# RMS norms of a two-layer streaming encoder: one product with ones, and an inverse root at full width

## The chip, the cores and the metric

The kernel runs on one core of a Trainium2 chip. The metric is device time in microseconds (us) of one execution; the times shown are medians of several executions. The core has five engines that work side by side, each through its own queue in order: TensorE (PE, matrix products, with its weight loads shown apart as PEld), VectorE (DVE), ScalarE (ACT), GpSimd (POOL) and SyncE (SP, which issues the DMAs here).

## The reference, cut to what matters

A prompt of 1024 frames and a running stream of 32 frames go through two layers with d_model 1024. Layer 0 mixes by a gated recurrence (HGRN2), layer 1 by a sliding-window attention; both have a SwiGLU feed-forward part. Around each of these four parts stands an RMS norm on the way in and one on the way out, and the second layer's keys and values have a weight vector of their own on the same normalised x:

```python
def rms_norm(x, w):
    xf = x.astype(F32)
    y = xf * lax.rsqrt(jnp.mean(xf * xf, axis=-1, keepdims=True) + NORM_EPS)
    return (y * w.astype(F32)).astype(x.dtype)
...
for layer in range(DEPTH):
    h = rms_norm(x, norm_mix_pre[layer])
    ...
    x = x + rms_norm(mix, norm_mix_post[layer])
    hf = rms_norm(x, norm_ffn_pre[layer])
    a, b = jnp.split(hf @ w_ffn_in[layer], 2, axis=-1)
    x = x + rms_norm((jax.nn.silu(a) * b) @ w_ffn_out[layer], norm_ffn_post[layer])
```

In the recurrence each head's output has a norm over its 128 values too (`o = rms_norm(o, g_norm) * silu(g)`).

## The kernel before, in words

Activations lie transposed: the 1024 features in eight groups of 128 partitions, the 1056 frames along the free dimension in three blocks b = 0, 1, 2 of 384, 384 and 288 columns (`BL`). Each dense product splits both operands into a high and a low part (`wh`, `wl`, `xh`, `xl`) and adds three products, so eight feature groups make 24 matrix products into one PSUM tile (`mm_fm`, L133; `mm_tm` with frames on the output partitions, L145; `fmul`, L495, for the second feed-forward matrix). The PSUM pool of these tiles, `mmps()`, has four buffers. Weights come by DMA on SP into `wst` and are split by ACT (`wh`, L98 or L102) and DVE (`wl`, L99 or L103).

A norm needs, for each frame (column), the sum of squares over 1024 features, that is over eight groups and 128 partitions. `sq_acc` squares each group on ACT (L171, L174) and adds the groups on POOL (L175) into `acc`. Then come two steps:

- `rstd`: three products with blocks of 128 columns of `acc` as weights and one column of ones (L181) give the sums with frames on partitions, a tile of 128x3. `newton` (L152 to L161) makes the inverse root of it on DVE: 12 instructions on three columns, a first guess from the bits and three Newton steps. The result `r` (tiles `r2`, `rt`) is also what the products with frames on partitions use as scale of a row: in `vproj` (L702), `gproj` (L717, L718) and `vproj1` (L1121).
- `rbcast`: DVE makes a diagonal matrix `dm` from `ident` and `r` (L186), one product with ones as weights puts r on all partitions (L190), and ACT copies it from PSUM (L191) to `rb` or `rb2`, which scales columns.

There are 24 norms over d_model: three at the load of x (`xload`), and for each of the four parts and three blocks one of the part's output (in `postnorm`, with `rb2`), and one of the new x (in `postnorm`, with `rb`) except behind the last part. So twelve are of outputs and twelve of x. `gproj` uses `newton` too, on six columns, twelve times.

`postnorm` and the others are Python generators: a `yield` ends a piece, and the caller asks for pieces (`go`, `step`, `run`) between dense products, so the text gives an order of work in which norms and dense products interleave. `after_dense()` puts a norm's product in PE's queue behind the last dense product written before it. The tile framework then fixes each engine's order before the run by its own plan, in which an instruction that is ready in the plan may go ahead of one written earlier; on the chip each engine keeps to that order. In the first feed-forward part the second half of `postnorm` of block 2 goes on into the projections of the next layer (`go(f0)`).

Of the kernel before, what the change touches and what calls it, by code (L numbers as in the profile page):

```python
# [18 lines left out]
D = 1024  # L19
# [40 lines left out]
def build(nc, tc, I, O):  # L60
# [16 lines left out]
    def tt(tag, bufs):  # L77
        return tp.tile([128, 384], F32, tag=tag, name=tag, bufs=bufs)

    def mmps():  # L80
        return pm.tile([128, 512], F32, tag="mm", name="mm")
# [70 lines left out]
    def newton(dst, ss, n, cnt, wtag):  # L152
        v = tp.tile([128, n], F32, tag=wtag + "v", name="nv", bufs=2)
        t = tp.tile([128, n], F32, tag=wtag + "t", name="nt", bufs=2)
        nc.vector.tensor_scalar(v, ss, 1.0 / cnt, EPS, mult, add)
        nc.vector.tensor_scalar(dst.bitcast(I32), v.bitcast(I32), -0.5, float(0x5f3759df), mult, add)
        nc.vector.tensor_scalar(v, v, -0.5, None, mult)
        for _ in range(3):
            nc.vector.tensor_tensor(t, dst, dst, mult)
            nc.vector.tensor_tensor(t, t, v, mult)  # L160
            nc.vector.scalar_tensor_tensor(dst, t, 1.5, dst, add, mult)  # L161

    def newacc(b):
        acc = tt("acc", 3)
        if BL[b][1] < 384:
            nc.gpsimd.memset(acc[:, BL[b][1]:], 1.0)
        return acc
# [9 lines left out]
    def rstd(acc, r, ps=None):  # L177
        ps = mmps() if ps is None else ps
        with after_dense():
            for j in range(3):  # L180
                nc.tensor.matmul(ps[:, j:j + 1], acc[:, j * 128:(j + 1) * 128], ones[:, 0:1], start=True, stop=True)  # L181
        newton(r, ps[:, 0:3], 3, D, "n3")

    def rbcast(dst, r, W, ps=None):
        dm = tt("dm", 1).rearrange("p (a b) -> p a b", a=3)
        nc.vector.tensor_tensor(dm, ident.unsqueeze(1).broadcast_to([128, 3, 128]),  # L186
                                r.unsqueeze(2).broadcast_to([128, 3, 128]), mult)
        ps = mmps() if ps is None else ps
        with after_dense():
            nc.tensor.matmul(ps[:, :W], ones, dm.rearrange("p a b -> p (a b)")[:, :W], start=True, stop=True)  # L190
        nc.scalar.copy(dst[:, :W], ps[:, :W])  # L191
# [17 lines left out]
    def postnorm(b, mix, acc, w2, xold, wnext, spill, yout, done, more=None, full=None):  # L209
# [16 lines left out]
        r2 = tp.tile([128, 3], F32, tag="r2", name="r2", bufs=2)  # L226
        rstd(acc, r2)
        yield
        rb2 = tt("rb2", 1)
        rbcast(rb2, r2, W)  # L230
# [19 lines left out]
        if yout is None:  # L250
# [3 lines left out]
            r = cp.tile([128, 3], F32, tag=f"rt{b}", name=f"rt{b}")  # L254
            rstd(nacc, r)
            yield
            rb = cp.tile([128, W], F32, tag=f"rb{b}", name=f"rb{b}")
            rbcast(rb, r, W)
# [16 lines left out]
    def ffn(L, nx, post1, post, wmix, v1, w2, xold, wnext, spill, yout, res):  # L275
# [231 lines left out]
        def step(b):  # L507
            if b not in ts:
                c0, W = BL[b]

                def done(*r):
# [4 lines left out]
                                 lambda: mp.tile([128, 384], F32, tag="xo", name="xo", bufs=3))  # L516
# [130 lines left out]
    with tc.tile_pool(name="hp", bufs=1) as hp, \  # L647
# [4 lines left out]
        def xload(b, mid=None):  # L652
# [17 lines left out]
            yield  # L670
            r = rts[b] = cp.tile([128, 3], F32, tag=f"rt{b}", name=f"rt{b}")
            rstd(acc, r, hps.tile([128, 512], F32, tag="po", name="po", bufs=1) if b == 0 else None)
            yield
            rb = rbs[b] = cp.tile([128, W], F32, tag=f"rb{b}", name=f"rb{b}")
            rbcast(rb, r, W, hps.tile([128, 512], F32, tag="hs", name="hs", bufs=1) if b == 0 else None)
# [30 lines left out]
        def gproj(p, b):  # L706
# [3 lines left out]
            newton(ro, ssq[p, b], 6, 128, "n6")  # L710
# [13 lines left out]
        def stage_a(c, h, b):  # L724
# [16 lines left out]
            if h == b == 0:  # L741
                go(xl0)
                go(v0, 2)
                go(xl0)
            rb = rbs[b]
# [708 lines left out]
```

## Time and profile before

| | |
|---|---|
| median of 3 runs | 2577.68 us (2573.69 to 2578.14) |
| the profiled execution | 2575.38 us |
| its span, first to last instruction | 2573.6 us |
| PE, PEld busy | 2484.7, 2388.2 us (97%, 93%) |
| DVE, ACT, POOL busy | 1695.1, 1074.3, 453.9 us (66%, 42%, 18%) |
| chain that ended last | PE 77%, DVE 12%, ACT 4%, DMA 3% |
| mean granted TensorE clock | 0.986 |

How to read it: a row of a group names line, engine, operation, what is written and read (`out<-in`), the shape, the number of instructions, then busy time and mean ns of one, and the idle time of the engine before them with what ended it. A row of the timeline has the start and duration in us, and in brackets the idle time before it. [...] Products are pipelined and the ends of their records are modelled, so what a product costs PE is read from the distance of two starts. A row of waits says who waited for whom, us in total, how often, and the longest.

The dense work is steady from 725 to 1300 us and from 1880 to 2460 us (the first feed-forward matrices of the two layers). The recurrence fills the first 625 us, the attention 1480 to 1800.

### The profile page before, as it was taken

What the parts mean: (1) busy time and instruction counts of PE and PEld (TensorE: products, weight loads), DVE (VectorE), ACT (ScalarE), POOL (GpSimd) and SP (SyncE); (2) the same over time, 40 slices, a digit from 0 to 9 for tenths busy, and PEclk for the clock granted to TensorE, in tenths of its full rate; (3) what the DMA queues carried; (4) which work ended last, traced back from release to release, by engine and by line L of the source; (5) the groups of instructions that cost most, each with busy time, mean ns of one, the idle gap of its engine ahead of it and who ended that gap; (6) DMA issues with size and microseconds to landing.
All of it is one profiled execution on the core that took longest, in us unless ns stands there. A gap on an engine that the chain in (4) does not pass through costs nothing.

```text
span 2573.6 us, 44368 instructions
## 1 busy us (share of the span) xinstructions
PE 2484.7 (97%) x17232; PEld 2388.2 (93%) x17232; DVE 1695.1 (66%) x3694; ACT 1074.3 (42%) x2323; POOL 453.9 (18%) x652
## 2 busy tenths in 40 slices
PE   7999998999999999999998999989999999999997
PEld 7999998998899999999998997768899999999997
DVE  8787779888676666552467647687776666652455
ACT  6555655656433333342344324555433333342332
POOL 5543434332200000000034311121300000000021
PEclk9999999999999999999999999999999999999998
DMA  5333333443422222252455542223422222252454
GB/s 169 91 100 99 119 100 124 131 129 120 137 80 83 75 75 75 80 172 75 149 164 173 168 140 75 68 79 100 147 81 82 75 75 75 78 174 75 150 172 144
DMA packets 124155, 288.01 MB, mean 112 GB/s; under 512 B 13432, under 2 KB 68632, under 8 KB 123944
## 3 DMA queue, kind: packets, MB, share of 16 engines
q1 hardware_dynamic: 123944, 285.17, 35.1%
q8 instruction: 135, 2.21, 0.4%
q14 instruction: 76, 0.62, 0.1%
HBM read 237.25 MB, written 48.07 MB: 111 GB/s over the span
## 4 chain that ended last, share of the span: by engine, by line
PE 77%; DVE 12%; ACT 4%; DMA 3%; issue 2%; POOL 2%; SPq 0%; POOLq 0%; ACTq 0%; DVEq 0%
PE mm L133 28%; PE mm L495 17%; PE mm L404 15%; PE c L404 6%; PE mm L145 5%; DVE wl L103 2%; PE sc L1218 1%; PE pav L1276 1%; ACT wh L102 1%; PE ptp L1258 1%; DVE wl L99 1%; PE mm L190 1%; DVE mixb L240 1%; DMA xl<-g 1%; DVE mixb L239 1%
## 5 line engine op out<-in xcount | busy, mean ns | idle before, releaser
L133 PE MATMUL mm<-xh,wh 128*128 128x384 f32 (+1 forms) x1968 | 634.4, 323 | 8.1 <-ACT xh L206 7.1
L133 PE MATMUL mm<-xh,wl 128*128 128x384 f32 (+1 forms) x1968 | 626.5, 318 | 12.2 <-DVE wl L103 8.4
L133 PE MATMUL mm<-xl,wh 128*128 128x384 f32 (+1 forms) x1968 | 628.6, 319 | 1.0 <-DVE xl L207 0.8
L175 POOL TENSOR_TENSOR acc<-acc,tmp 128x384 f32<-128x384 f32 (+1 forms) x168 | 212.0, 1266 | 1724.6 <-ACT tmp L174 1721.3
L103 DVE TENSOR_TENSOR wl<-wst,wh 128x1024 fp32r<-128x1024 f32 (+1 forms) x301 | 377.2, 1255 | 183.2 <-ACT wh L102 182.3
L102 ACT CAST wh<-wst 128x1024 fp32r<-128x1024 f32 (+1 forms) x301 | 314.0, 1046 | 398.4 <-PE mm L495 231.8
L133 PEld LDWEIGHTS mm<-xh,wl 128*128 128x128 f32 x1968 | 373.4, 190 | 20.0 <-DVE wl L103 9.3
L133 PEld LDWEIGHTS mm<-xh,wh 128*128 128x128 f32 x1968 | 374.1, 190 | 15.2 <-ACT xh L206 7.1
L133 PEld LDWEIGHTS mm<-xl,wh 128*128 128x128 f32 x1968 | 373.9, 190 | 9.9 <-issue 3.9
L495 PE MATMUL mm<-xh,wl 128*128 128x384 f32 (+1 forms) x768 | 247.5, 322 | 1.7 <-DVE wl L103 1.7
L495 PE MATMUL mm<-xl,wh 128*128 128x384 f32 (+1 forms) x768 | 247.5, 322 | 0.0
L495 PE MATMUL mm<-xh,wh 128*128 128x384 f32 (+1 forms) x768 | 247.1, 322 | 0.0
L145 PE MATMUL mm<-wh,xh 128*128 128x256 f32 (+1 forms) x648 | 185.6, 287 | 1.9 <-ACT vt L702 1.9
L145 PE MATMUL mm<-wh,xl 128*128 128x256 f32 (+1 forms) x648 | 183.2, 283 | 0.0
L145 PE MATMUL mm<-wl,xh 128*128 128x256 f32 (+1 forms) x648 | 182.6, 282 | 0.0
L388 ACT CAST sh<-sr 128x512 fp32r<-128x512 f32 x144 | 89.5, 622 | 175.6 <-PE mm L404 147.9
L495 PEld LDWEIGHTS mm<-xh,wl 128*128 128x128 f32 x768 | 144.2, 188 | 2.1 <-DVE wl L103 2.1
L495 PEld LDWEIGHTS mm<-xh,wh 128*128 128x128 f32 x768 | 144.1, 188 | 0.0
L495 PEld LDWEIGHTS mm<-xl,wh 128*128 128x128 f32 x768 | 144.1, 188 | 0.0
L145 PEld LDWEIGHTS mm<-wh,xh 128*128 128x128 f32 (+1 forms) x648 | 119.0, 184 | 3.5 <-ACT vt L702 2.1
L145 PEld LDWEIGHTS mm<-wh,xl 128*128 128x128 f32 (+1 forms) x648 | 119.0, 184 | 0.8
L145 PEld LDWEIGHTS mm<-wl,xh 128*128 128x128 f32 (+1 forms) x648 | 118.5, 183 | 0.5
(278 smaller groups left out, 5113.3 us busy)
## 6 DMA issues: line engine op xcount, KB each, us to landing
wst<-in_wfo SPq DMA_DIRECT2D x92, 512.0 KB
wst<-in_wfi SPq DMA_DIRECT2D x88, 512.0 KB
wst<-in_wfq SPq DMA_DIRECT2D x47, 512.0 KB
g<-u SPq DMA_DIRECT2D x72, 192.0 KB
wst<-in_wi SPq DMA_DIRECT2D x24, 512.0 KB
wst<-in_wg SPq DMA_DIRECT2D x24, 512.0 KB
wst<-in_wao SPq DMA_DIRECT2D x24, 512.0 KB
xl<-g SPq DMA_DIRECT2D x32, 384.0 KB
```

Source lines behind the costliest of these rows:

```text
L99: nc.vector.scalar_tensor_tensor(wl[:, s], st[:, s], pcol(name, k0 + k), wh[:, s].bitcast(F32), mult, sub)
L102: nc.scalar.copy(wh[:, s], st[:, s])
L103: nc.vector.tensor_tensor(wl[:, s], st[:, s], wh[:, s].bitcast(F32), sub)
L133: last_mm[0] = nc.tensor.matmul(ps[:, :W], w, x, start=i == 0, stop=i == n - 1)
L145: last_mm[0] = nc.tensor.matmul(ps[:rows, :256], x, w, start=i == 0, stop=i == n - 1)
L175: nc.gpsimd.tensor_tensor(acc[:, :W], acc[:, :W], q[:, :W], add)
L190: nc.tensor.matmul(ps[:, :W], ones, dm.rearrange("p a b -> p (a b)")[:, :W], start=True, stop=True)
L239: nc.vector.scalar_tensor_tensor(m, m, pcol(w2, k), rb2[:, :W], mult, mult)
L240: nc.vector.tensor_tensor(m, m, xos[k][:, :W], add)
L388: nc.scalar.copy(h, r)
L404: last_mm[0] = nc.tensor.matmul(ps[:, :384], a, c, start=start and k == i == 0, stop=k == 3 and i == 2, skip_group_check=True)
L495: last_mm[0] = nc.tensor.matmul(ps[:, :W], a, c[:, q, :], start=start and q == i == 0, stop=stop and q == f - 1 and i == 2, skip_group_che ...
```

## The change

`rstd` and `rbcast` go. `rnorm` makes one product with ones (128x128) as weights and all columns of `acc`, which gives the sums on all partitions at once, and `rsqrt` makes the inverse root there at the width of the block: v = ss/1024 + eps and two squares and one linear step on ACT, the first guess and five more instructions on DVE, with a step of third order and a Newton step. The tile `dm` goes, and u, an intermediate, is written into the norm's PSUM tile by ACT. Where a scale of rows is needed (at the load of x, and with `tok=True` behind the first feed-forward part), `rcol` takes it out of the full-width result by products with one column of `ident` and a copy on DVE. `gproj` uses `rsqrt` with all steps on DVE. The columns of `acc` beyond a block's width aren't set to one any more. At the first head, `rcol` and the second piece of `vproj` change places with the broadcast.

```diff
-    def newton(dst, ss, n, cnt, wtag):
-        v = tp.tile([128, n], F32, tag=wtag + "v", name="nv", bufs=2)
-        t = tp.tile([128, n], F32, tag=wtag + "t", name="nt", bufs=2)
-        nc.vector.tensor_scalar(v, ss, 1.0 / cnt, EPS, mult, add)
+    def rsqrt(dst, ss, v, t, u, cnt, sq, lin):
+
+        lin(v, ss, 1.0 / cnt, EPS)
         nc.vector.tensor_scalar(dst.bitcast(I32), v.bitcast(I32), -0.5, float(0x5f3759df), mult, add)
-        nc.vector.tensor_scalar(v, v, -0.5, None, mult)
-        for _ in range(3):
-            nc.vector.tensor_tensor(t, dst, dst, mult)
-            nc.vector.tensor_tensor(t, t, v, mult)
-            nc.vector.scalar_tensor_tensor(dst, t, 1.5, dst, add, mult)
+        sq(t, dst)
+        nc.vector.tensor_tensor(t, t, v, mult)
+        lin(u, t, 0.375, -1.25)
+        nc.vector.tensor_tensor(t, u, t, mult)
+        nc.vector.scalar_tensor_tensor(dst, t, 1.875, dst, add, mult)
+        sq(t, dst)
+        nc.vector.scalar_tensor_tensor(t, t, -0.5, v, mult, mult)
+        nc.vector.scalar_tensor_tensor(dst, t, 1.5, dst, add, mult)
...
     def newacc(b):
-        acc = tt("acc", 3)
-        if BL[b][1] < 384:
-            nc.gpsimd.memset(acc[:, BL[b][1]:], 1.0)
-        return acc
+        return tt("acc", 3)
...
-    def rstd(acc, r, ps=None):
+    def rnorm(acc, dst, W, ps=None):
+
         ps = mmps() if ps is None else ps
         with after_dense():
-            for j in range(3):
-                nc.tensor.matmul(ps[:, j:j + 1], acc[:, j * 128:(j + 1) * 128], ones[:, 0:1], start=True, stop=True)
-        newton(r, ps[:, 0:3], 3, D, "n3")
-
-    def rbcast(dst, r, W, ps=None):
-        dm = tt("dm", 1).rearrange("p (a b) -> p a b", a=3)
-        nc.vector.tensor_tensor(dm, ident.unsqueeze(1).broadcast_to([128, 3, 128]),
-                                r.unsqueeze(2).broadcast_to([128, 3, 128]), mult)
+            nc.tensor.matmul(ps[:, :W], ones, acc[:, :W], start=True, stop=True)
+        v, t = tt("nv", 1), tmp()
+        rsqrt(dst[:, :W], ps[:, :W], v[:, :W], t[:, :W], ps[:, :W], D,
+              lambda o, x: nc.scalar.activation(o, x, AF.Square),
+              lambda o, x, m, a: nc.scalar.activation(o, x, AF.Copy, bias=a, scale=m))
+
+    def rcol(dst, W, r, ps=None):
+
         ps = mmps() if ps is None else ps
+        n = (W + 127) // 128
         with after_dense():
-            nc.tensor.matmul(ps[:, :W], ones, dm.rearrange("p a b -> p (a b)")[:, :W], start=True, stop=True)
-        nc.scalar.copy(dst[:, :W], ps[:, :W])
+            for j in range(n):
+                rows = min(128, W - j * 128)
+                nc.tensor.matmul(ps[:rows, j:j + 1], dst[:, j * 128:j * 128 + rows], ident[:, 0:1], start=True,
+                                 stop=True)
+        nc.vector.tensor_copy(r[:, :W // 128], ps[:, :W // 128])
+        if W % 128:
+            nc.vector.tensor_copy(r[:W % 128, n - 1:n], ps[:W % 128, n - 1:n])
...
@@ postnorm @@
-        r2 = tp.tile([128, 3], F32, tag="r2", name="r2", bufs=2)
-        rstd(acc, r2)
+        rb2 = tt("rb2", 1)
+        rnorm(acc, rb2, W)
         yield
-        rb2 = tt("rb2", 1)
-        rbcast(rb2, r2, W)
         yield
...
-            r = cp.tile([128, 3], F32, tag=f"rt{b}", name=f"rt{b}")
-            rstd(nacc, r)
+            r = None
+            rb = cp.tile([128, W], F32, tag=f"rb{b}", name=f"rb{b}")
+            rnorm(nacc, rb, W)
             yield
-            rb = cp.tile([128, W], F32, tag=f"rb{b}", name=f"rb{b}")
-            rbcast(rb, r, W)
+            if tok:
+                r = cp.tile([128, 3], F32, tag=f"rt{b}", name=f"rt{b}")
+                rcol(rb, W, r)
...
@@ xload @@
+            rb = rbs[b] = cp.tile([128, W], F32, tag=f"rb{b}", name=f"rb{b}")
+            rnorm(acc, rb, W, hps.tile([128, 512], F32, tag="po", name="po", bufs=1) if b == 0 else None)
+            yield
             r = rts[b] = cp.tile([128, 3], F32, tag=f"rt{b}", name=f"rt{b}")
-            rstd(acc, r, hps.tile([128, 512], F32, tag="po", name="po", bufs=1) if b == 0 else None)
-            yield
-            rb = rbs[b] = cp.tile([128, W], F32, tag=f"rb{b}", name=f"rb{b}")
-            rbcast(rb, r, W, hps.tile([128, 512], F32, tag="hs", name="hs", bufs=1) if b == 0 else None)
+            rcol(rb, W, r, hps.tile([128, 512], F32, tag="hs", name="hs", bufs=1) if b == 0 else None)
...
@@ stage_a @@
             if h == b == 0:
                 go(xl0)
-                go(v0, 2)
+                go(v0)
                 go(xl0)
+                go(v0)
```

More of the change, by code (lines that the diff above doesn't have):

```diff
@@ L207, in put_x, with postnorm @@
             nc.vector.scalar_tensor_tensor(xl[:, k, :], src, pcol(wname, k), xh[:, k, :].bitcast(F32), mult, sub)
-    def postnorm(b, mix, acc, w2, xold, wnext, spill, yout, done, more=None, full=None):
+    def postnorm(b, mix, acc, w2, xold, wnext, spill, yout, done, more=None, full=None, tok=False):
         W = BL[b][1]
@@ L515, in step @@
                                  None if spill is None else spill[b], None if yout is None else yout[b], done,
-                                 lambda: mp.tile([128, 384], F32, tag="xo", name="xo", bufs=3))
+                                 lambda: mp.tile([128, 384], F32, tag="xo", name="xo", bufs=3), tok=True)
             next(ts[b], None)
@@ L709, in gproj @@
             ro = hp.tile([128, 6], F32, tag="ro", name="ro", bufs=2)
-            newton(ro, ssq[p, b], 6, 128, "n6")
+            nv, nt, nu = [hp.tile([128, 6], F32, tag=t, name=t, bufs=2) for t in ("nv", "nt", "nu")]
+            rsqrt(ro, ssq[p, b], nv, nt, nu, 128, lambda o, x: V.tensor_tensor(o, x, x, mult),
+                  lambda o, x, m, a: V.tensor_scalar(o, x, m, a, mult, add))
             for jl in range(3):
```

## The prediction

> **What bounds the kernel now.** I read the first lines of the page first (busy shares, then the chain that ended last), then the table of stages, then TensorE's waits and the instructions of the norms one by one.
>
> ```profile
> span 2573.6 us, 44368 instructions
> PE 2484.7 (97%) x17232; PEld 2388.2 (93%) x17232; DVE 1695.1 (66%) x3694; ACT 1074.3 (42%) x2323; POOL 453.9 (18%) x652
> PE 77%; DVE 12%; ACT 4%; DMA 3%; issue 2%; POOL 2%; SPq 0%; POOLq 0%; ACTq 0%; DVEq 0%
> ```
>
> The chain lies on TensorE (PE) for 77% of the span and on VectorE (DVE) for 12%. So an instruction taken from PE's queue is worth its slot there, and a DVE instruction costs only where PE waits for it. The span is 2573.6 us in an execution of 2575.38 us; 1.8 us lie around it. The median of the runs shown is 2577.68, 2.3 us above this execution.
>
> ```profile
> 725.00:1300.00 575.00, 573.93 (x3581) 572.96 (x3580) 321.03 (x503) 186.16 (x284) 7.89 (x5) 1.00 0.30 95
> 1300.00:1480.00 180.00, 167.39 (x1065) 163.64 (x1064) 128.46 (x251) 72.21 (x141) 71.46 (x59) 0.97 0.55 171
> ```
>
> The stages: window, then busy time of PE, PEld, DVE, ACT and POOL. Inside a feed-forward stage (the first row) PE idles 1 us of 575, and no norm falls there. The 24 norms stand at the joints, as in the second row, where PE idles 12.6 us of 180. The page's waits name one cause that belongs to the norms:
>
> ```profile
> PE mm L190 <- DVE dm L186: 18.8, 11, 4.7
> ```
>
> PE stood 18.8 us in 11 places before a broadcast product, waiting for the diagonal matrix.
>
> **The change part by part.** *The sums.* Each norm now issues three products with one column, from the squares, and each shows as two records:
>
> ```profile
> L181 PE MATMUL mm<-ones,acc x138: 164/250/353, 118.3 to 2558.6; 128*128 128x1 f32 x138
> L190 PE MATMUL mm<-dm,ones x46: 403/484/1010, 139.9 to 2562.4; 128*128 128x384 f32 x30, 128*128 128x288 f32 x16
> ```
>
> With the first norm's six in another tile that is 24 norms of six records; the second row is the broadcast, two records each. The slot of one such six, in PE's own order:
>
> ```profile
> 1312.52 0.34 PE L495 MATMUL mm<-xh,wl 128*128 128x384 f32 x1
> 1312.69 0.72 PE L181 MATMUL mm<-ones,acc 128*128 128x1 f32 x6
> 1313.28 0.42 PE L495 MATMUL mm<-gh,wh 128*128 128x384 f32 x1
> 1313.53 0.34 PE L495 MATMUL mm<-gl,wh 128*128 128x384 f32 x1
> 1313.71 0.35 PE L495 MATMUL mm<-gh,wl 128*128 128x384 f32 x1
> ```
>
> Dense products start 0.17 apart. Without the six, the third one behind would have started at 1312.69 + 2 x 0.175 = 1313.04 instead of 1313.71: 0.67 us. The product with ones that replaces them has the shape of today's broadcast product, so the new sum takes over the broadcast's slot and costs nothing extra. In six norms (three at the load of x, three behind the first feed-forward part) rcol brings back three one-column products, so those six keep their 0.67. Of the 18 that lose it, the last one is on the tail and counted there: 17 x 0.67 = **-11.4 us**.
>
> *The wait for dm.* In 18 norms PE's queue no longer holds a product that needs DVE's result. Of the 18.8 us, these places are not simply given back:
>
> ```profile
> 28.86 0.39 PE L145 MATMUL mm<-wh,xh 128*128 128x256 f32 x1 [1.86 <-ACT vt L702]
> 29.08 0.81 PE L190 MATMUL hs<-dm,ones 128*128 128x384 f32 x2
> 679.53 1.30 PE L190 MATMUL mm<-dm,ones 128*128 128x288 f32 x2 [2.84 <-DVE dm L186]
> 1417.48 1.65 PE L190 MATMUL mm<-dm,ones 128*128 128x384 f32 x2 [4.69 <-DVE dm L186]
> 1466.63 0.72 PE L190 MATMUL mm<-dm,ones 128*128 128x288 f32 x2 [1.41 <-DVE dm L186]
> 1797.22 0.88 PE L190 MATMUL mm<-dm,ones 128*128 128x384 f32 x2 [1.31 <-DVE dm L186]
> 1361.39 0.56 DVE L186 TENSOR_TENSOR dm<-ident,rt 128x384 f32<-128x384 f32 x1
> 1362.79 0.81 PE L190 MATMUL mm<-dm,ones 128*128 128x384 f32 x2
> ```
>
> 4.69 and 1.41 belong to norms with rcol, where PE's queue will stand behind the new inverse root instead; 2.88 is the tail's (below). 18.8 - 4.69 - 1.41 - 2.88 = 9.8 us could go. Behind the 1.31 at 1797 DVE itself leads (below), so I leave it: **-8.5 us**; ends 0 and -9.8. What is late next there is the weight halves wl; if they are, the first rival holds.
>
> *The clock behind a stall.* After the 2.84 stall at 679.5 the granted clock (the third column from the end) is low; behind the same place of the second layer it is not:
>
> ```profile
> 680.00:700.00 20.00, 20.00 (x100) 19.71 (x100) 11.27 (x25) 7.12 (x17) 4.13 (x5) 0.86 0.43 134
> 1840.00:1860.00 20.00, 19.50 (x113) 19.42 (x114) 13.34 (x27) 8.14 (x19) 4.74 (x6) 1.00 0.45 138
> ```
>
> 0.14 of 20 us is 2.8 us; **-2 us**, ends 0 and -2.8. [...]
>
> *The new inverse root.* Today 12 DVE instructions on three columns, then dm; afterwards four ACT and six DVE instructions at full width, handing over between the engines seven times. Durations at 384 columns:
>
> ```profile
> L191 ACT COPY rb<-mm 128x384 f32<-128x384 f32 x15 | 7.0, 470 | 11.3 <-PE mm L190 11.3
> L174 ACT ACTIVATE tmp<-mix 128x384 f32<-128x384 f32 x42 | 20.8, 517 | 1.2 <-DVE mix L564 1.1
> L749 DVE TENSOR_SCALAR F<-tmp,oml,lb 128x384 f32<-128x384 f32 x16 | 7.7, 479 | 7.8 <-ACT tmp L748 7.8
> L747 DVE TENSOR_TENSOR tmp<-mm,rb 128x384 f32<-128x384 f32 x16 | 8.9, 554 | 9.9 <-PE mm L133 9.8
> L186 DVE TENSOR_TENSOR dm<-ident,r 128x384 f32<-128x384 f32 x12 | 6.7, 558 | 0.4
> L268 DVE SCALAR_TENSOR_TENSOR mixb<-mixb,pv,rb 128x384 f32<-128x384 f32 x16 | 9.0, 615 | 1.1 <-ACT rb L191 1.1
> ```
>
> v and u on ACT 2 x 0.47, two squares 0.52, the bit step 0.48, two products 0.56 and 0.55, three fused steps 0.62: 5.4 us, with ten hand-overs of 0.03 to 0.09 (rows of the tail) 5.9. No row has ACT writing PSUM, as u does; its nearest rows are the reads of PSUM (0.47) and SBUF squares (0.52), ends 0.4 and 0.6, and I take 0.47. Before that comes the sum's product, 0.81 + 0.04: the scale is on all partitions **6.7 us** after the sum starts. Today, undisturbed:
>
> ```profile
> 662.84 0.15 DVE L155 TENSOR_SCALAR nv<-mm 128x3 f32<-128x3 f32 x1
> 665.06 0.56 DVE L186 TENSOR_TENSOR dm<-ident,rt 128x384 f32<-128x384 f32 x1
> ```
>
> 0.76 for the sums, 2.78 from nv to the end of dm: dm stands after 3.5 us and rb after 4.9 (0.81 + 0.47 + hand-overs). So rb comes 1.8 us later, and where PE waits (dm now, rb at rcol then) 3.2 us later.
>
> *rcol.* The kernel's second norm has its sums at 118.3 and its broadcast at 139.9 (the first starts in the rows of L181 and L190), the third is like it: nothing. Four are exposed: the start and those with broadcasts at 1363, 1417 and 1467. At 1363 dm ended 0.84 us before its product; at 1417 and 1467 PE stood already. Each can lose 0 to 3.2 us; the order on an engine is planned, so a product that is planned later stands further back and shows no stall. I take the middle, 4 x 1.6 = **+6.4 us**, ends 0 and +12.8. At the start, one run of 24 vproj products and the copy of vt are also moved behind rcol (no DMA is among them: the weights are requested in the first piece). The broadcast at 29.08 stands between the first and second product of such a run, so the plan puts what is ready first; the cost is in the 0 to 3.2.
>
> *DVE-led joints.* At the second block's residual norm of either layer (1797 and its twin in the first) what follows waits for DVE, and there POOL's additions lengthen DVE's instructions:
>
> ```profile
> 1810.66 2.45 DVE L239 SCALAR_TENSOR_TENSOR mixb<-mixb,pv,rb 128x384 f32<-128x384 f32 x2
> 1807.36 7.70 POOL L175 TENSOR_TENSOR acc<-acc,tmp 128x384 f32<-128x384 f32 x6
> ```
>
> 2.45 for two instead of 2 x 0.615. Two norms 1.8 us late: **+3 us**, ends 0 and +3.7.
>
> *The tail.* All of the last norm is on the path:
>
> ```profile
> 2558.06 0.83 PE L181 MATMUL mm<-ones,acc 128*128 128x1 f32 x6 [2.02 <-POOL acc L175]
> 2558.93 0.16 DVE L155 TENSOR_SCALAR nv<-mm 128x3 f32<-128x3 f32 x1 [2.39 <-PE mm L181]
> 2559.12 0.17 DVE L156 TENSOR_SCALAR r<-nv 128x3 int32<-128x3 int32 x1
> 2561.16 0.56 DVE L186 TENSOR_TENSOR dm<-ident,r 128x384 f32<-128x384 f32 x1
> 2561.77 1.33 PE L190 MATMUL mm<-dm,ones 128*128 128x288 f32 x2 [2.88 <-DVE dm L186]
> 2563.14 0.40 ACT L191 COPY rb<-mm 128x288 f32<-128x288 f32 x1 [6.07 <-PE mm L190]
> 2563.57 0.52 DVE L239 SCALAR_TENSOR_TENSOR mix<-mix,pv,rb 128x288 f32<-128x288 f32 x1 [1.85 <-ACT rb L191]
> ```
>
> 5.5 us from the sums to L239. Afterwards: one product of 288 columns, 0.7 (shape of 1466.63) to 1.33 us, say 1.0; the ten steps 5.4 x 0.40/0.47 = 4.6; hand-overs 0.4: 6.0. **+0.5 us**, ends +0.2 and +0.9.
>
> *At nothing:* the eight POOL memsets of the unused columns; two DVE instructions fewer in each of twelve gproj calls; one buffer of PSUM held until u is read (some 3.5 us, while a dense product of 24 fills the next in 4.2). Cover: PE's dense work; without it the last would cost what is left of those 3.5 us at one joint.
>
> **The sum.** -11.4 - 8.5 - 2 + 6.4 + 3 + 0.5 = -12.0: 2563.4 for this execution, 2565.7 from the median. I say 2565.
>
> **The rivals.** *The stalls come back.* PE leaves dm, and meets the late weights or wl a little later; then only the slots remain, -11.4, with +6.4 + 3 + 0.5 against them: -1.5, 2576. For it: DVE and DMA are busiest at these joints (128 of 180 us). Against: PE has a whole product of 4.2 us to start on at 679.5.
>
> *PE's queue stands behind rcol: slower.* Each of the ten hops can find a longer instruction ahead of it on its engine, and ACT's casts wait for weights from DMA. Without rcol's losses the change gains 18.4 us; over four norms it turns at 4.6 us more than today each. All ten hops behind half an instruction of 0.6 us are 3.0, on top of 3.2: 6.2 x 4 = 24.8, so +6.4, 2584. Against: the small instructions of today have just as many hops.
>
> *POOL blocks the wide steps.* The fourth term at every exposed norm: four of the six DVE steps read two operands from SBUF, each 0.6 us longer under POOL's additions, 2.4 us at the six exposed joints: 14.4, so +2.4, 2580. POOL is busy 71 of 180 us in the joint shown. [...]
>
> **The numbers.** Forecast 0.68 (its own range 2556 to 2572), stalls back 0.17, rcol 0.08, POOL 0.07. A measurement here tells 0.2%, 5 us, from no change: the forecast is faster, the first rival the same, rcol slower, and POOL's lies near the bound and is halved between the two: 0.68, 0.20, 0.12. The range 2554 to 2578 has the best ends of all terms (-11.4 - 9.8 - 2.8 + 0.2, -23.8) below and the first rival above.
>
> **What would show it.** One product with ones of 384 columns per norm and 36 one-column records instead of 144; no wait for dm; stalls before rcol at the four exposed norms of no more than 8 us; no stall where the one of 2.84 stands, in either layer; from the last sum to L239 about 6 us. It is wrong if PE waits longer in front of rcol than that, or if PE's idle time outside the norms grows by what the slots gave.

## The result, and the profile after

The changed kernel takes **2580.93 us** (median of 22 runs, 2574.22 to 2587.17) against 2575.85 (22 runs, 2572.41 to 2582.65) for the kernel before beside it: ratio 1.0018, 95% interval 1.001 to 1.0027, so some 5 us slower, at the edge of what the prediction called no change. The forecast was 12 us faster. The profiled execution is one of the longer ones, 2586.45 us.

The first lines of its page:

```profile
span 2584.7 us, 44049 instructions
PE 2487.6 (96%) x17124; PEld 2387.2 (92%) x17124; DVE 1704.8 (66%) x3510; ACT 1104.9 (43%) x2395; POOL 444.7 (17%) x644
...
PE 61%; DVE 9%; DMA 4%; ACT 3%; issue 2%; POOL 0%; SPq 0%; POOLq 0%; DVEq 0%; ACTq 0%
```

DVE has 184 instructions fewer and is busy 10 us longer, ACT 31 us longer: narrow steps have become wide ones. The new norm's products, by line:

```profile
L180 PE MATMUL mm<-acc,ones 128*128 128x384 f32 (+1 forms) x46 | 19.3, 503 | 10.3 <-POOL acc L174 10.3
L193 PE MATMUL mm<-ident,rb x30: 164/250/373, 142.5 to 1475.5; 128*128 128x1 f32 x26, 128*32 128x1 f32 x4
L193 PE MATMUL hs<-ident,rb x6: 250/250/272, 31.1 to 31.7; 128*128 128x1 f32 x6
```

The 144 one-column records have become 36, as the change says. TensorE's waits (who waited for whom, us in total, times, longest):

```profile
PE mm L180 <- POOL acc L174: 10.3, 4, 3.8
PE po L973 <- DVE Sq L947: 9.4, 7, 2.7
PE mm L193 <- DVE rb L163: 8.5, 3, 5.1
...
PE hs L193 <- DVE rb L163: 3.4, 1, 3.4
```

The 18.8 us for `dm` are gone. In their place PE waits 11.9 us for `rb` before the products of `rcol`, and longer for the sums of squares (10.3 against 4.5) and for `Sq` of the recurrence (9.4 against 7.0). At 680, where the 2.84 us stall stood, the window that had 0.86 now has a full clock:

```profile
680.00:700.00 20.00, 20.00 (x117) 19.89 (x116) 18.71 (x40) 9.88 (x23) 1.36 (x2) 1.00 0.23 77
```

To see where time went, I compared when PE starts the n-th dense product in either trace. (The times are those of the kernel before.) Up to 645 us the changed kernel falls 10.6 us behind (3.0 of it by 53 us, 5.4 between 535 and 570, 4.6 between 612 and 645), wins 6.2 back by 691, loses 9.6 from 1340 to 1481 (the joint of the two layers) and 5.4 from 1638 to 1745, of which 3.5 come back by 1800. The kernel before with only its tiles moved (e14, a run further down) also lost 4.1 at 1638 to 1745, so most of that piece is the scatter of one execution. The windows of the joint, 830 or so products in each:

```profile
1340.00:1481.00 141.00, 128.39 (x841) 124.91 (x840) 99.65 (x204) 54.96 (x114) 60.16 (x51) 0.96 0.56 173
```

```profile
1340.00:1491.00 151.00, 132.93 (x831) 129.57 (x830) 101.94 (x175) 62.82 (x130) 56.63 (x51) 0.93 0.54 165
```

The first is the kernel before, the second the changed one. Idle time grows from 12.6 to 18.1 us, and the clock falls from 0.96 to 0.93: 5.5 us and about 4.9 (0.07 x 151 - 0.04 x 141). So about half of the loss there is not waiting but the slower clock.

### The profile page after: what moved, and what is told of

Its sections match the earlier page's. It is cut to its first block, busy times and chain, and to the rows that moved or that the text cites. A ratio compares the mean times of both kernels' runs of the same rounds, so it can differ in the third digit from the quotient of the medians.

```text
span 2584.7 us, 44049 instructions
## 1 busy us (share of the span) xinstructions
PE 2487.6 (96%) x17124; PEld 2387.2 (92%) x17124; DVE 1704.8 (66%) x3510; ACT 1104.9 (43%) x2395; POOL 444.7 (17%) x644
## 4 chain that ended last, share of the span: by engine, by line
PE 61%; DVE 9%; DMA 4%; ACT 3%; issue 2%; POOL 0%; SPq 0%; POOLq 0%; DVEq 0%; ACTq 0%
PE mm L133 20%; PE mm L501 15%; PE mm L410 14%; PE c L410 6%; DVE wl L103 2%; PE mm L145 2%; PE sc L1227 1%; PE pav L1285 1%; ACT wh L102 1%; DMA wst<-in_wfo 1%; PE ptp L1267 1%; DVE xl L210 1%; DMA xl<-g 1%; DVE mix L244 1%; DVE wl L99 1%
## 5 line engine op out<-in xcount | busy, mean ns | idle before, releaser
L174 POOL TENSOR_TENSOR acc<-acc,tmp 128x384 f32<-128x384 f32 (+1 forms) x168 | 204.0, 1219 | 1737.4 <-ACT tmp L173 1734.4
L133 PEld LDWEIGHTS mm<-xl,wh 128*128 128x128 f32 x1968 | 373.9, 190 | 11.2 <-DVE xl L213 5.1
```

The lines of the kernel that those rows point to most:

```text
L133: last_mm[0] = nc.tensor.matmul(ps[:, :W], w, x, start=i == 0, stop=i == n - 1)
L174: nc.gpsimd.tensor_tensor(acc[:, :W], acc[:, :W], q[:, :W], add)
```

## The experiments

The letters of the theories are not the same throughout: in the first runs A lays the loss on the row scale, and B says that what PE is spared comes back as other waits; from the ninth run on B means what its expectation says. "Ratio" is against the kernel before, run beside it; 0.1% is 2.6 us. Against their expectations e2, e3, e6, e7 and e8 moved further than forecast, e5 lies between its two ranges, and e9 and e12 came out slower than either of theirs.

### What the parts cost

**e4: the one-column products doubled** in 21 norms of the kernel before.

```diff
-            for j in range(3):
+            for j in [0, 1, 2] * times:
```

> The kernel before with the three one-column products issued twice in the 21 norms behind the load of x: 126 more records on PE, nothing else. It prices the slots. If a slot of 0.67 us on PE is worth 0.67 us of the span, 13 to 15 us slower than before, 2589 to 2591. If PE's queue has slack at these joints (Theory B), 0 to 5 us slower, 2576 to 2581.

2590.37 us, ratio 1.0063 (1.0045 to 1.008): +14.5 after the kernel before beside it (2575.84), 0.69 for each set of six records. The slots of the prediction (0.67) are real time. How much of the 14.5 is the slots themselves is open, though: the mean granted clock of these six runs was 0.984, that of the kernel before beside them 0.987.

**e3: the wide root cut short**, its linear step and the bit step left. The kernel leaves out the refinement, so its scale is a first guess; the scratch tile of the root goes too.

```diff
         nc.vector.tensor_scalar(dst.bitcast(I32), v.bitcast(I32), -0.5, float(0x5f3759df), mult, add)
+        if cnt == D:
+            return
```

> The changed kernel with the wide inverse root cut to the linear step on ACT and the bit step on DVE; the eight refining steps of the norms over d_model are left out. The scale then stands some 2 us after the sum instead of 6.4 to 18.9. If the length of the root (its ten hand-overs, each behind other work) is what eats the gain, this shows the gain that was forecast and more: 2552 to 2566 us, with stalls in front of rcol under 1.5 us each. Theory B: the stalls appear elsewhere, 2573 to 2580.

2537.19 us, ratio 0.9857 (0.9838 to 0.9876): 44 us less than the changed kernel. By the mean durations of their rows the eight steps last some 4.2 us in each norm, 101 us in all 24. Dense work lies beside many of them, and 44 us are what the kernel pays.

**e5: the same steps issued, but nobody waits for them.**

```diff
+        o = v if cnt == D else dst
...
-        nc.vector.scalar_tensor_tensor(dst, t, 1.875, dst, add, mult)
+        nc.vector.scalar_tensor_tensor(o, t, 1.875, o, add, mult)
```

> The changed kernel with every instruction of the wide root still issued, but the refining steps of the norms over d_model write a scratch tile: consumers take the unrefined scale (the refinement is left out of the outputs). The short root has shown that the eight steps cost 38.6 + 5.1 = 44 us in 24 norms. If that is the wait for the result (latency), this kernel is near the short root: 2537 to 2550 us. If it is the time that the steps take on DVE and ACT at joints where these engines lead (occupancy), it stays near the changed kernel: 2570 to 2581.

2559.09 us, ratio 0.9945 (0.9929 to 0.9961). Half of the 44 us is gone, half is left: about 22 us are waiting for the chain's end, and about 22 the place that the steps take on DVE and ACT ahead of other work.

**e6: linear steps and squares on DVE too.**

```diff
-              lambda o, x: nc.scalar.activation(o, x, AF.Square),
-              lambda o, x, m, a: nc.scalar.activation(o, x, AF.Copy, bias=a, scale=m))
+              lambda o, x: nc.vector.tensor_tensor(o, x, x, mult),
+              lambda o, x, m, a: nc.vector.tensor_scalar(o, x, m, a, mult, add))
```

> The changed kernel with the two linear steps and the two squares of the wide root on DVE as well: ten DVE instructions in a row, no hand-over between engines. Latency through hand-overs behind ACT's queue: 3 to 10 us faster than the changed kernel, 2571 to 2578. Occupancy of DVE: four more wide DVE instructions per norm, some 2 us, at about ten joints that DVE leads, 2595 to 2605.

2613.66 us, ratio 1.0153 (1.0133 to 1.0172): +33 against the changed kernel for 96 wide DVE instructions more, although the hand-overs between the engines inside the root go. DVE's time at the joints is dear, not the hand-overs. Part of the price is paid through TensorE's clock: the mean granted clock of these runs was 0.974, against 0.982 of the changed kernel.

**e2: only the six norms with a row scale new**, the other 18 (and `gproj`) as before.

```diff
+            if tok:
+                rnorm(nacc, rb, W)
+            else:
+                rstd(nacc, r)
```

> The complement: only the six norms with a scale of rows have the change, the other 18 and the gproj root are as before. Theory A: all of the loss and none of the gain, 2583 to 2590 us. Theory B: little changes, 2576 to 2580.

2591.4 us, ratio 1.0061 (1.0043 to 1.0079): +15.5.

**e1: the reverse**, the six as before and the other 18 new.

```diff
-            rnorm(nacc, rb, W)
+            if tok:
+                rstd(nacc, r)
+            else:
+                rnorm(nacc, rb, W)
```

> The six norms that also need a scale of rows (three at the load of x, three behind the first feed-forward part) keep the one-column sums, the narrow inverse root, the diagonal matrix and the broadcast; the other 18 have the change. Theory A (the loss is rcol: PE's queue stands behind the wide inverse root in exactly these six, and the change is worth having in the other 18): 8 to 12 us faster than the changed kernel, 2566 to 2571 us, and the stalls of 3.4, 1.2, 5.1 and 2.3 us in front of rcol become the old ones. Theory B (what PE is spared in the 18 comes back as other waits, for weight halves, POOL's sums and DVE): like the changed kernel within 3 us, 2576 to 2582.

2579.52 us, ratio 1.0015 (1.0004 to 1.0026). The expected gain did not come, and it does not fit e2: +15.5 for the six and +3.7 for the 18 should make +19, and the whole change makes +5. Something else differed between these kernels.

### What did not fit

**e9: the two norms ahead of `L274` as before** (block 0's second norm behind the attention or recurrence output in either layer). In the changed kernel DVE stands there behind a reload by DMA (start, duration, and in brackets the idle time with what ended it):

```profile
542.58 0.62 DVE L274 SCALAR_TENSOR_TENSOR xo<-xo,pv,rb 128x384 f32<-128x384 f32 x1 [1.26 <-DMA xo<-xsa]
...
545.61 0.92 DVE L274 SCALAR_TENSOR_TENSOR xo<-xo,pv,rb 128x384 f32<-128x384 f32 x1 [1.24 <-DMA xo<-xsa]
...
548.37 0.33 DVE L947 SCALAR_TENSOR_TENSOR Sq<-state,D,pu 128x128 f32<-128x128 f32 x1
...
548.76 0.80 PE L973 MATMUL po<-Sq,Q 128*128 128x128 f32 x2 [2.71 <-DVE Sq L947]
```

In the kernel before, `Sq` stands at 541.37, and the first of these scalings (L268 there) starts behind it:

```profile
541.37 0.33 DVE L938 SCALAR_TENSOR_TENSOR Sq<-state,D,pu 128x128 f32<-128x128 f32 x1
...
550.36 0.60 DVE L268 SCALAR_TENSOR_TENSOR xo<-xo,pv,rb 128x384 f32<-128x384 f32 x1
```

Its scale came out of a broadcast product that stood behind dense work in PE's queue; without that product the plan takes the scalings early, ahead of `Sq`, and on the chip the reload is not there yet.

```diff
+            if full == "back":
+                r = cp.tile([128, 3], F32, tag=f"rt{b}", name=f"rt{b}")
+                rstd(nacc, r)
+                yield
+                rbcast(rb, r, W)
+            else:
+                rnorm(nacc, rb, W)
+                yield
```

> Two of the 24 norms (block 0's second norm after the attention output in either layer, whose rows are normalised from reloaded tiles) take the narrow root, the diagonal matrix and the broadcast product of the kernel before; the other 22 stay new. Theory B (the new form lets the plan place the reload-bound row scalings of block 0 ahead of Sq on VectorE, at 531 to 546 us, and TensorE loses about 5 us between 535 and 570 us): that loss goes, the stretch of 34.3 us in the kernel before is again within 1 us of it, and the run takes 2576 to 2578 us (-5, +1.3 for two slots). Rival (the loss there is the scatter of one execution, or comes from an earlier norm): the stretch still takes 4 us or more longer than before, and the time is 2580 to 2583.

At the place it came as expected: the stretch from 535 to 570 us is 0.53 us longer than in the kernel before, where the changed kernel lost 5.42. The time did not follow: 2585.34 us, ratio 1.0037 (1.0023 to 1.0051).

**e12: less work, more time.** The shorter wide root (e7, below) with a shorter six-column root in `gproj`:

```diff
-            rsqrt(ro, ssq[p, b], nv, nt, nu, 128, lambda o, x: V.tensor_tensor(o, x, x, mult),
-                  lambda o, x, m, a: V.tensor_scalar(o, x, m, a, mult, add))
+            newton(ro, ssq[p, b], 6, 128, "n6")
```

> The seven-instruction wide root in all 24 norms, and in the twelve calls of six columns a narrow root of eight DVE instructions instead of ten. If occupancy of VectorE by these small instructions counts, 24 instructions of 0.15 us less at most: 2549 to 2552 us; if they lie beside other work, the 2552 us of the wide root alone.

2560.62 us, ratio 0.9946 (0.9933 to 0.9958), 8 us more than e7 with 24 instructions fewer. Its trace loses 12 us against e7, 9 of them between 725 and 1340 us and from 1875 on, mostly steady stretches without a norm.

### The weight tiles' place in SBUF

So I looked at the steady stretch itself: 700 dense products of the first layer's second feed-forward matrix (1180.1 to 1295.0 us in the kernel before). PE waits for nothing there, and yet their total, from the records' start times, has one of three values, the same to a nanosecond in all kernels that share it (a row of the window shows it as a count of products in 115 us):

- 114.573 us: the changed kernel, e3, e5, e6, e7 (and e10, e11 below)
- 114.883 us: the kernel before, e2, e4, e8 (below)
- 115.783 us: e1, e9, e12

```profile
1180.00:1295.00 115.00, 115.00 (x704) 1.00 0.33 108
```

```profile
1180.00:1295.00 115.00, 115.00 (x702) 1.00 0.33 109
```

```profile
1180.00:1295.00 115.00, 115.00 (x698) 1.00 0.32 107
```

These are the changed kernel, the kernel before and e9; the clock is 1.00 in all. What goes with the value is where the weight tiles (`wh`, `wl`) lie: the norms' small tiles stand ahead of them in SBUF, and each edit of the root moves them. In the programs the first `wh` starts at byte 115392 of a partition in the kernel before, at 115072 in the changed one, and at 115200 in e1 and e9. The remainder by 256 is 128 at the first value, 192 at the second and 0 at the third, in all fourteen kernels. Five kernels were run again with nothing but an unused tile ahead of the weights:

```diff
     wp = ctx.enter_context(tc.tile_pool(name="wp", bufs=1))
+    gap = wp.tile([128, 32], F32, name="gap")
+    nc.gpsimd.memset(gap, 0.0)
```

(48 columns instead of 32 in e14.)

**e13**

> The changed kernel with an unused tile of 128 bytes per partition ahead of the weight tiles, which moves them from byte 115072 to 115200 (remainder by 256 from 128 to 0). Theory C (the offset of the weight tiles sets the rate of dense products): the 700 products that took 114.57 us take 115.78, and the run 2588 to 2592 us. Rival (the rate goes with the instructions or the plan, not with the offset): 114.57 again, and 2579 to 2583.

2590.34 us, ratio 1.0052 (1.0038 to 1.0067); the 700 products take 115.783 us.

**e14**

> The kernel before with an unused tile of 192 bytes ahead of the weight tiles, which moves them from byte 115392 to 115584 (remainder by 256 from 192 to 128, that of the changed kernel). Theory C: the 700 products that took 114.88 us take 114.57, and the run 2570 to 2573 us; the difference of the changed kernel to this one, some 9 us, is then what the change costs without the move. Rival: 114.88 and 2574 to 2577.

The 700 products take 114.573 us, as expected, but the time is 2577.25 us, ratio 0.9996 (0.9984 to 1.0009): the rate moved, and the 4 us that it should be worth can't be told from nothing. Only the step to remainder 0 is large enough to be seen in the time.

**e15**

> The six row norms on the old path and the other 18 new, with an unused tile of 128 bytes that moves the weight tiles from byte 115200 (remainder 0) to 115328 (remainder 128). Theory C: 114.57 us for the 700 products instead of 115.78, and 2568 to 2572 us, so that the row scale costs about 10 us at one and the same offset, which the unshifted run hid. Rival: 2578 to 2581 as unshifted, and the row scale costs nothing.

2566.92 us, ratio 0.9962 (0.9948 to 0.9976), 114.573 us.

**e16**

> The two norms ahead of reloaded row scalings on the old path and the other 22 new, with an unused tile of 128 bytes that moves the weight tiles from remainder 0 to 128. Theory C: 114.57 us for the 700 products instead of 115.78, and 2574 to 2577 us, so that the 5 us given back between 535 and 570 us are seen in the time as well. Rival: 2583 to 2586 as unshifted.

2574.11 us, ratio 0.999 (0.998 to 1.0), 114.573 us.

**e18**: e12 with the unused tile.

> The seven-instruction wide root in all 24 norms and the eight-instruction narrow root in the twelve calls of six columns, with an unused tile of 128 bytes that moves the weight tiles from remainder 0 to 128. By the offset: 114.57 us for the 700 products instead of 115.78, and 2550 to 2553 us, that of the run with the wide root alone (2552.4). If the six-column root itself costs the 8 us, 2558 to 2562.

2553.35 us, ratio 0.9912 (0.9892 to 0.9933), 114.573 us: that of e7 again.

In all five the rate is that of the new place. Where remainder 0 came or went, the four ratios differ by 0.34, 0.53, 0.47 and 0.34%, on average 11 us of 2577. The starts of products of 384 columns in e13:

```profile
1204.40 0.34 PE L503 MATMUL mm<-xh,wh 128*128 128x384 f32 x1
1204.59 0.34 PE L503 MATMUL mm<-xl,wh 128*128 128x384 f32 x1
1204.76 0.34 PE L503 MATMUL mm<-xh,wl 128*128 128x384 f32 x1
1204.93 0.34 PE L503 MATMUL mm<-xh,wh 128*128 128x384 f32 x1
1205.11 0.34 PE L503 MATMUL mm<-xl,wh 128*128 128x384 f32 x1
1205.29 0.34 PE L503 MATMUL mm<-xh,wl 128*128 128x384 f32 x1
```

At this place the distances run 173, 175, 175, 181, 176 ns and over again (173, 174, 175, 182, 176 in e9), 175.9 on average; at remainder 128 nearly all are 173 or 174. Why is not shown, nor whether it is the weights themselves or one of the tiles behind them, which move along.

### At one and the same place

With that, e1 and e9 can be read. Against e14, the kernel before at the changed kernel's remainder, the 18 norms of e15 gain 0.34%, **-8.8 us** (±5, from the two intervals). From e15 to the whole change the six norms with a row scale lose 0.56%, **+14.4** (±4), as in e2 (+15.5, both sides at remainder 192). The sum is +5.6, and the changed kernel stands 0.22% above e14. And the two norms ahead of `L274`, e16 against the changed kernel, are worth 0.28%, **7.2** (±3.4).

The traces bear out both places. From 1340 to 1481 us five kernels with the six row norms and the root as in the change (the changed kernel, e2, e9, e13, e16) take 6.2 to 9.6 us longer than the kernel before; e1, e14, e15 and e17, with these norms as before, lie between 2.2 us less and 0.5 more. And the two norms ahead of `L274` have a second place, from 612 to 645 us. In three pairs that differ by them alone (the changed kernel and e16, e15 and e17, e10 and e11) this stretch is 4.6, 4.6 and 4.3 us longer than in the kernel before with them new, and 0.1, 0.0 and -0.5 with them as before. (Not every kernel with them new loses it: e7 and e12 lose 0.4 and 0.0, e18 4.2.) First the kernel before, then the changed one:

```profile
612.00:645.00 33.00, 32.91 (x232) 30.42 (x231) 28.97 (x77) 21.90 (x58) 7.34 (x8) 1.00 0.40 130
```

```profile
612.00:645.00 33.00, 31.98 (x190) 27.64 (x189) 20.50 (x64) 19.35 (x57) 1.00 (x1) 0.84 0.22 71
```

The clock is 0.84 there, although the longest wait of PE in this stretch is 0.92 us; what lowers it is not shown.

**e17: both taken back**, 16 norms new.

```diff
+            elif full == "back":
+                r = cp.tile([128, 3], F32, tag=f"rt{b}", name=f"rt{b}")
+                rstd(nacc, r)
...
-            if tok:
+            if tok or full == "back":
                 rbcast(rb, r, W)
```

> Sixteen norms new; the six with a row scale and the two ahead of reloaded row scalings as before; weight tiles at remainder 128. If the two losses are separate, 2566.9 - 7 = 2560 us (2557 to 2563), near the forecast of the whole change without its term for the row scale (2565.7 - 6.4 = 2559) although two slots are given up; PE's stretch between 535 and 570 us is within 1 us of the kernel before, and no wait for a row scale's products is left. If they overlap (one takes the place of the other), 2564 to 2568.

2563.07 us, ratio 0.9946 (0.9928 to 0.9964): against e14 -12.9 us (±5.7). It is at the upper edge of the range for separate losses; the two may overlap by a few us.

What a norm with a row scale loses is seen in the third exposed one. First the changed kernel, then e15:

```profile
1415.04 0.81 PE L180 MATMUL mm<-acc,ones 128*128 128x384 f32 x2
...
1418.09 0.47 ACT L184 ACTIVATE nv<-mm 128x384 f32<-128x384 f32 x1
1419.73 0.35 DVE L155 TENSOR_SCALAR rb<-nv 128x384 int32<-128x384 int32 x1
...
1424.91 0.55 DVE L163 SCALAR_TENSOR_TENSOR rb<-tmp,rb 128x384 f32<-128x384 f32 x1
...
1425.51 1.44 PE L193 MATMUL mm<-ident,rb 128*128 128x1 f32 x6 [5.08 <-DVE rb L163]
...
1427.60 0.52 PE L133 MATMUL mm<-xh,wl 128*128 128x384 f32 x1
1427.92 0.52 PE L133 MATMUL mm<-xh,wh 128*128 128x384 f32 x1
```

```profile
1404.49 0.72 PE L219 MATMUL mm<-ones,acc 128*128 128x1 f32 x6
1407.24 0.14 DVE L170 TENSOR_SCALAR nv<-mm 128x3 f32<-128x3 f32 x1
...
1411.22 0.56 DVE L224 TENSOR_TENSOR nv<-ident,rt 128x384 f32<-128x384 f32 x1
...
1411.84 0.91 PE L228 MATMUL mm<-nv,ones 128*128 128x384 f32 x2 [1.59 <-DVE nv L224]
```

10.4 us from the sums to the scale against 7.3 to the diagonal matrix (which lies in the tile `nv` in e15). In both cases the next engine came late to the sums (ACT by 2.2 us, DVE by 2.0), and in the wide chain ACT and DVE did other work between the steps. PE stood 5.08 us instead of 1.59. And behind the stall the dense products start 0.32 us apart instead of 0.17, for the next 5 us. The windows behind it (the third number from the end is the clock), again the changed kernel first:

```profile
1426.00:1440.00 14.00, 14.00 (x67) 13.89 (x68) 6.93 (x16) 1.72 (x4) 3.88 (x4) 0.79 0.25 78
```

```profile
1411.00:1425.00 14.00, 13.16 (x73) 12.79 (x74) 12.34 (x26) 5.29 (x13) 4.38 (x4) 1.00 0.36 125
```

0.21 of 14 us is 2.9 us. Behind the other three stalls before `rcol` (3.44 at 27.7, 1.16 at 1364.7, 2.31 at 1472.6 us) the windows of the changed kernel are:

```profile
31.00:45.00 14.00, 13.13 (x76) 13.05 (x77) 12.82 (x29) 8.38 (x16) 8.68 (x16) 0.88 0.34 97
1364.00:1378.00 14.00, 12.84 (x83) 12.26 (x82) 6.33 (x10) 5.00 (x8) 1.63 (x1) 0.88 0.32 103
1474.00:1490.00 16.00, 15.07 (x95) 15.05 (x96) 9.02 (x21) 3.46 (x9) 6.97 (x8) 0.89 0.42 119
```

That is 5.1 us more (the second may belong to a stall of 3.79 before the sums at 1352); in e15 the clock is 1.00 behind all four places. So four stalls, 12.0 us, and up to 8.0 us of missing clock (2.9 and 5.1). In e15 there are two stalls at these places, 1.59 and 1.64 us, so the stalls grow by 8.8 us.

These windows are of one execution each, and the kernel before has a low clock at two of the places as well (0.91 from 31 to 45 us, 0.82 from 1417.5 to 1432). But the granted clock of every run is on record. (1 - granted clock) x span is what the missing clock would cost a TensorE that is busy throughout: 10 us at a clock of 0.5 count 5. The mean over the runs of a kernel, with twice its standard error:

| kernel | runs | missing clock, us |
|---|---|---|
| before, beside the experiments | 73 | 35.4 ± 1.0 |
| e14, before, moved | 12 | 35.8 ± 2.8 |
| e17, 16 norms new | 6 | 35.4 ± 3.8 |
| e15, 18 norms new | 6 | 40.2 ± 1.8 |
| e16, 22 norms new | 12 | 43.5 ± 1.8 |
| e2, six row norms new | 6 | 45.3 ± 4.0 |
| the changed kernel | 22 | 46.2 ± 2.0 |

Within one and the same kernel a run with 1 us more of it took 0.67 us longer (fitted over all 215 runs). So the 10.8 us of missing clock that the changed kernel has more than the kernel before are worth some 7 to 11 us, an estimate: at the old clock it would be 2 to 6 us faster than before. From e15 to the whole change the clock makes 6.0 us at most, and with the 8.8 us of stalls that is about the 14.4 measured.

### Shorter roots

**e7: the wide root in seven steps**, the first guess from the bits of the raw sums and two Newton steps with fitted constants, without v and u (eps enters in the steps alone).

```diff
+        nc.vector.tensor_scalar(zb.bitcast(I32), p.bitcast(I32), -0.5, MAGIC, mult, add)
+        nc.scalar.activation(t, zb, AF.Square, scale=S1)
+        nc.vector.scalar_tensor_tensor(t, p, EPS * D, t, add, mult)
+        nc.vector.scalar_tensor_tensor(zb, t, -C1, zb, add, mult)
+        nc.scalar.activation(t, zb, AF.Square, scale=S2)
+        nc.vector.scalar_tensor_tensor(t, p, EPS * D, t, add, mult)
+        nc.vector.scalar_tensor_tensor(zb, t, -C2, zb, add, mult)
```

> The changed kernel with a wide root of seven instructions instead of ten: first guess from the bits of the sums in PSUM, two Newton steps with fitted constants (three instructions each: square on ACT, product with the sums plus 1024 eps, fused last step, on DVE), no v and no u. Eight steps cost 44 us, 5.5 each; three fewer on the path give 16 us: 2561 to 2569, faster than both kernels. If only DVE's time counts, one instruction of five fewer gives 9 us: 2572.

2552.37 us, ratio 0.992 (0.9897 to 0.9944): 29 us less than the changed kernel, three steps less in 24 norms.

**e8: the kernel before with eight narrow steps instead of twelve**, by the same constants.

```diff
+        for a, c in ((0.522883469677355, 1.5233504518360352), (0.5, 1.5000004746954132)):
+            nc.vector.scalar_tensor_tensor(t, dst, a, dst, mult, mult)
+            nc.vector.tensor_tensor(t, t, v, mult)
+            nc.vector.scalar_tensor_tensor(dst, t, -c, dst, add, mult)
```

> The kernel before with its root on three columns cut from 12 DVE instructions to 8 (the same two fitted Newton steps). Each dm stands 0.8 us earlier; of 18.8 us in 11 waits up to 8 us go: 2567 to 2572. If the waits are only moved, 2574 to 2577.

2560.77 us, ratio 0.9948 (0.993 to 0.9965). Four instructions of 0.16 us less in each of 36 calls (24 on three columns, twelve on six) are worth 14 us over the kernel.

**e10 and e11: each root in its place.** e10 has the wide root of e7 in 18 norms, and the narrow one of e8 with the broadcast in the six with a row scale and in `gproj`; e11 the narrow one also in the two norms ahead of `L274`. Both lie at remainder 128. The edits are those of e1, e7, e8 and e17 together.

> The seven-instruction wide root (two fitted Newton steps straight from the sums) in 18 norms; the six norms that need a row scale, and the twelve of six columns, take a narrow root of eight instructions with the diagonal matrix. If the stalls before the row scale's products (2.2 + 0.8 + 3.9 + 1.5 us in the run with the wide root everywhere) go and the narrow root with dm costs TensorE less than that, 2545 to 2550 us; if six slots of 0.67 us and the waits for dm take the gain back, 2551 to 2555.

> The kernel with the short wide root in 18 norms and the narrow one in six, where the two norms ahead of reloaded row scalings take the narrow root as well (16 and eight). By Theory B 1 to 2 us less than with 18 and six, since the short wide root lost only 1.8 us between 535 and 570 us, less two slots of 0.67: within 1.5 us of it. By the rival (no early placing) 1.3 us more.

e10 2542.94 us, ratio 0.988 (0.9862 to 0.9898); e11 **2541.77 us**, ratio 0.9867 (0.9852 to 0.9883), the fastest of all, 33 us below the kernel before. The stretch from 535 to 570 us is 5.58 us longer than before in e10 and 0.56 in e11, so the place behaves as in e9; that the time gains from it is not resolved here.

## Why the prediction was wrong, point by point

- *The slots*, -11.4: right by e4 (0.69 each), as far as its 14.5 us are slots.
- *The wait for dm and the clock behind it*, -8.5 and -2: the waits went, the window at 680 has its full clock, and the dense products between 645 and 691 us take 6.2 us less. Right at the place that could be read singly, but wrong for the kernel: the clock term was to give 2 us back, and over all runs the changed kernel has 10.8 us more of missing clock, worth 7 to 11. In the changed kernel's execution the clock is low behind the stalls of 5.08 us (0.79 from 1426 to 1440 us), 2.31 us (0.89 from 1474 to 1490) and, before `Sq`, 2.71 us (0.77 from 545 to 560); behind the 1.59 us of e15 it is 1.00 (1411 to 1425).
- *rcol*, +6.4: **the first step that failed**, +14.4. The stalls themselves are somewhat longer than forecast: 12.0 us at the four exposed norms, 5.9 more than the 4.69 and 1.41 of the kernel before and 8.8 more than in e15, and above the 8 us that the prediction named as its sign of being wrong. What the step left out is the clock: up to 6 us more of missing clock from e15 to the whole change. I had charged the low clock to the stall that goes, and not to the four that come or grow. "6.7 us after the sum" was an undisturbed chain: it took 9.9 us at the start, 10.4 in the rows above, and 11.2 at 1463.6.
- *What is late next*: **the second step that failed.** I looked for a later operand of the same product (the weights, `wl`) and named that as the first rival. But with the broadcast gone from PE's queue, the plan moved other work: the scalings of `L274` went ahead of `Sq` on DVE and waited for their DMA. 7.2 us, at places that the prediction does not name (535 to 570 and 612 to 645 us). `acc` came late to its product too (5.8 us more in the waits); no run takes that apart.
- *The 18 norms*: -18.4 forecast (without rcol), -8.8 measured; without the two at `L274` -17.1 forecast (two slots less) and -12.9 ± 5.7 measured. What is left of the miss is within the intervals. The clock has a part in this term too: e15 has 4.4 us more of missing clock than e14, e17 none.
- *DVE-led joints*, +3: not seen. From 1800 to 1875 us the changed kernel gains 1.8 us.
- *The tail*, +0.5: 5.49 us from the last sum to the scaling (below) against 5.51. With nothing in its way the wide chain of 288 columns is as short as the narrow one with its broadcast.

```profile
2569.37 0.75 PE L180 MATMUL mm<-acc,ones 128*128 128x288 f32 x2 [2.02 <-POOL acc L174]
...
2574.36 0.46 DVE L163 SCALAR_TENSOR_TENSOR rb<-tmp,rb 128x288 f32<-128x288 f32 x1
2574.86 0.95 DVE L243 SCALAR_TENSOR_TENSOR mix<-mix,pv,rb 128x288 f32<-128x288 f32 x2
```

- *At nothing*: the tiles that go moved the weight tiles, to a place that is a little faster in the steady stretch. It was in no term; its worth can't be told from nothing here (e14), and with the tiles 128 bytes further the change would have cost 0.34%, 8.8 us, more (e13).

Of the rivals, "PE's queue stands behind rcol" is the one that happened, with its sign and nearly its condition: it was to turn at 4.6 us more than today at each of four norms, and 14.4 is 3.6 each, with the gain on the other side smaller by the scalings of `L274`. It happened by another way than the rival had it, though: that counted stalls alone. "POOL blocks the wide steps" did not happen: of the 96 wide steps of the changed kernel that read two operands from SBUF, four lasted over 1 us (1.10 to 1.34), the others 0.44 to 0.68, and none of the four is at an exposed norm with a row scale.

## What to carry to other kernels

Price a stall with the clock behind it, both where a change takes stalls away and where it brings them: here 8.8 us of stalls came with some 6 us of missing clock. When a product leaves the queue, ask which work it had been holding back, and whether that work waits for something else. And before two versions are compared by a few tenths of a per cent, see whether a stretch that neither touches runs at the same rate in both.

## What the runs showed of the hardware

- The rate of dense products whose queue never waits went with the place of the weight tiles in SBUF, and of the tiles behind them, which move along: 173.4 ns for 384 columns at remainder 128 by 256 bytes, 175.9 on average and up to 182 in a pattern of five at remainder 0, at a granted clock of 1.00; between these two 9 to 14 us of a kernel of 2577 in four pairs. Remainder 64 was not run.
- Twelve instructions of 0.16 us on three columns are not nearly free: four of them fewer per call gave 14 us (e8). Whether by DVE's queue or by the chain to `dm` is not taken apart.
- Half of what the wide root's refinement costs stays when no one waits for it (e5): 22 us of the kernel's time, for steps on DVE and ACT, which have splits of weights to do beside them.
- One kernel's executions differ by their clock: 0.67 us of time for each us of (1 - granted clock) x span, over 215 runs. And a low clock does not need a long wait of PE: 0.84 from 612 to 645 us behind none above 0.92 us.
